# A hybrid decoder layer on one core: DRAM copies issued one behind each weight load, adding transfers one block to a step, and operand splits tied to places between products

## The chip, the cores and the metric

The kernel runs on one core of one Trainium2 chip. The metric is device time in microseconds, from the launch to the last instruction's end. The kernel before was timed in three runs: 650.31, 654.16 and 656.45 us, with a median of 654.16 us.

A core has five engines with a queue of instructions each, which run in the order of their queue and wait for each other by semaphores: TensorE (PE in the profile; its weight loads are PEld), VectorE (DVE), ScalarE (ACT), GpSimd (POOL) and SyncE (SP). SP only issues DMA transfers here; POOL and ACT issue some too.

## The reference

One layer over 512 tokens of width 1024, in float32:

```python
h = rms_norm(x, norm_g)
hq, hf, hi, hz, cq, ckv, kr, mz, glog = split(h @ w_in)
y_a = hgrn2(hq, hf, hi) with per-head rms_norm, * silu(hz)     # 8 heads of 128, chunks of 32
y_b = mla(cq, ckv, kr) * silu(mz)                              # 8 heads, causal softmax attention
gates = sigmoid(glog + b_gate)                                 # 512 x 2 x 1024
merged = gates[:, 0] * (y_a @ w_proj_a) + gates[:, 1] * (y_b @ w_proj_b)
x = x + merged @ w_out
return rms_norm(x, final_norm_g)
```

The 1024 x 1024 products for the two gates, for w_proj_a and for w_out are each done as seven products of half-size blocks instead of eight (a Strassen form). These need sums of weight blocks.

## The kernel before

**Precision.** A float32 operand is split into a high part (hi, rounded to the fast matmul type) and the rest (lo); each product is three matmuls, hi x hi, hi x lo and lo x hi. For weights, `load_w` (line 97) does this: SP issues the load of 512 KB into a raw buffer (three of them), ScalarE casts it to hi (line 113), VectorE subtracts to get lo (line 114); hi and lo have four buffers each. For other operands `split` (line 153) does the same two steps, and `a_parts` (line 826) calls it for two halves of a block.

**Stages.** First come the norm, the transposes and the small latent projections. Then four pairs of recurrent heads (`hg_pair`, line 562), each with weight loads for f (2), in every second pair i (4), q (2) and the gate z (2). In a pair, `hg_forget` and `hg_query` use VectorE and POOL, `hg_scores` and `hg_out` follow, and the norm's power runs on POOL. Then eight attention heads (line 893): scores with softmax, `mla_rope` for every second head, a gate, the next head's projections and the output. `mla_rope` (line 612) moves rows with DMAs from ScalarE's queue (qs<-qr, lines 618 and 625) with three POOL operations between. Its result qp is needed by the head's scores. Then come the two gates' products, the projection of branch a, all through `strassen` (line 867), then the projection of branch b, the product with w_out and the final norm.

**Block sums.** Class `BlockSums` (line 726) makes the weight sums in DRAM. For each of four matrices (the two gates', w_proj_a and w_out) there are four sum tensors t[0] to t[3] (g_t, pa_t and out_t in the profile). `start` (line 734) copies a block of the matrix into each, as two DRAM-to-DRAM transfers of 512 KB on SP's queue: eight to a matrix, 32 in all. `add` (line 740) adds a block or an earlier sum to one or more of them with adding transfers that POOL issues, two to a sum, 32 in all. t[0] and t[2] add blocks; t[1] adds t[0], and t[3] adds t[1].

**Where these stand.** `beside` (line 797) starts the first gate's copies after pair 0, the second's after pair 1 and pa's after pair 2; w_out's start with head 1 (line 920). The table `steps` (line 787) puts adds behind the f or q part of a pair (`step("f", pair)`, `step("q", pair)`) or behind a head (`step("h", h)`), with the sums 0 and 2 together. Six steps with adds lie in the pairs and six at the heads 1 to 6.

**The order.** The framework's scheduler orders each engine's instructions by its own model of their times. Inside `tc.manual_schedule` the named engines keep the order of the program. `tc.issue_after(ins)` makes the instructions traced in its block, of the engine that runs `ins`, stand behind `ins` in that engine's queue, with no wait. In `start`, these are the copies behind the last weight load traced; in `add`, POOL's issues behind `last_pool`, the last POOL operation of a head that has been noted.

**The gate stage.** Once the heads are done, the first gate's `strassen` runs (line 954). The branch's operands y11, y12 and y22 are then split into q1, q2 and q3, and four differences of blocks are made in `ya` (lines 955 to 962). The second gate's `strassen` has four more splits between its products (line 967), which write s1 to s4 once the products have read them. After it, eight splits of `yb` go into the space of hT (line 971), and the projection of branch a follows (line 981).

Of the kernel before, what the change touches and what calls it, by code (L numbers as in the profile page):

```python
# [9 lines left out]
F32 = mybir.dt.float32  # L10
# [4 lines left out]
ALU = mybir.AluOpType  # L15
# [8 lines left out]
H = 8  # L24
# [14 lines left out]
def hybrid_layer(ctx: ExitStack, tc: tile.TileContext, a):  # L39
# [55 lines left out]
    last_dma = [None]  # L95

    def load_w(*pieces, to=None):

        raw = wraw.tile([P, WCH], F32, tag="raw", name="w_raw")
        hi, lo = to or [pool.tile([P, WCH], F32R, tag=tag, name=f"w_{tag}")[:] for pool, tag in ((whi, "hi"), (wlo, "lo"))]  # L100
        views, o = [], 0
        for src in pieces:
            n = int(np.prod(src.shape[1:]))
            if len(src.shape) == 4:
                _, k, h, c = src.shape
                dst = raw[:, o : o + n].rearrange("p (k h c) -> p k h c", k=k, h=h)
                for i in range(k):
                    nc.sync.dma_start(dst[:, i], src[:, i])
            else:
                last_dma[0] = nc.sync.dma_start(raw[:, o : o + n].rearrange("p (k c) -> p k c", k=src.shape[1]), src)  # L110
            views.append([t[:, o : o + n].rearrange("p (k c) -> p k c", k=src.shape[1]) for t in (hi, lo)])
            o += n
        nc.scalar.copy(hi[:, :o], raw[:, :o])  # L113
        nc.vector.tensor_tensor(lo[:, :o], raw[:, :o], hi[:, :o].bitcast(F32), op=ALU.subtract)  # L114
        return views[0] if len(views) == 1 else views
# [42 lines left out]
    def power(out, x, mul, add, expo):  # L158

        nc.gpsimd.tensor_scalar(out, x, mul, add, op0=ALU.mult, op1=ALU.add)  # L160
        nc.gpsimd.tensor_tensor(out, out, expo, op=ALU.pow)
# [369 lines left out]
    def hg_out(h, asb, st_, q128, v_sb):  # L531
# [11 lines left out]
        power(ss[:], ss[:], 1.0 / P, 4 * EPS, neg_half)  # L543
# [18 lines left out]
    def hg_pair(pair, before_gate=None, last=None):  # L562
# [3 lines left out]
        step("f", pair)  # L566
# [15 lines left out]
        step("q", pair)  # L582
# [8 lines left out]
        def outs(aa):  # L591
            return [hg_out(h, aa[i], sts[i], qq[i][2], v_sb) for i, h in enumerate(hs)]
# [133 lines left out]
    class BlockSums:  # L726
# [7 lines left out]
        def start(self):  # L734
            with tc.issue_after(last_dma[0].ins):
                for t, ij in zip(self.t, TERMS):
                    for q in kh:
                        nc.sync.dma_start(t[:, q], self.w[ij][:, q])
# [22 lines left out]
    def early_sums(q):  # L761
# [9 lines left out]
        def keep(n, tag, src):  # L771
            hl = [ma_pool.tile([P, 2, 256], F32R, f"{tag}{i}") for i in range(2)]
            split(hl[0][:], hl[1][:], src)
            for i in range(2):
# [12 lines left out]
    steps = {("f", 0): lambda: early_sums(kh[0]),  # L787
             ("f", 1): lambda: gate_w[0].add(0, 2), ("q", 1): lambda: gate_w[0].add(1), ("f", 2): lambda: gate_w[0].add(3),
             ("q", 2): lambda: gate_w[1].add(0, 2), ("f", 3): lambda: gate_w[1].add(1), ("q", 3): lambda: gate_w[1].add(3),
             ("h", 1): lambda: pa_w.add(0, 2), ("h", 2): lambda: pa_w.add(1), ("h", 3): lambda: pa_w.add(3),  # L790
             ("h", 4): lambda: out_w.add(0, 2), ("h", 5): lambda: out_w.add(1), ("h", 6): lambda: out_w.add(3)}

    def step(*at):
        if at in steps:
            steps[at]()

    def beside(pair):
        if pair < 2:
            gate_w[pair].start()
        if pair == 0:  # L800
            early_sums(kh[1])
        if pair == 2:
            pa_w.start()

    for pair in range(H // 2 - 1):
        hg_pair(pair)
        beside(pair)
# [59 lines left out]
    def strassen(w, ops, out, pool, first=None, between={}):  # L867

        y11, y12, y22, s1, s2, s3, s4 = ops
        run = lambda n: between[n]() if n in between else None  # L870
        if first is None:
            u = ch_product(w.block(0, 0), y11, copied("c11", 1.0, pool))
            ch_product(w.block(1, 0), y12, closed("c11", 0, 0, 1.0, out), tile=mm_tile)
        else:
            u = first
# [17 lines left out]
    for h in range(H):  # L893
# [22 lines left out]
        elif h:  # L916
            late = (h, hook(), v, z)
            step("h", h)
            if h == 1:
                out_w.start()  # L920
        else:
            with tc.manual_schedule(engines={mybir.EngineType.PE}):
                nope = mla_nope(1, pools[1])
                v = mla_values(0)
                late = (0, hook(), v, z)
# [26 lines left out]
    h_ops = (h11, h12, h22, s1, s2, s3, s4)  # L952
    with tc.manual_schedule(engines={mybir.EngineType.PE}):
        strassen(gate_w[0], h_ops, gate_out(0, lambda j: ma[:, j]), gp, first=u)
    y11, y12, y21, y22 = blocks(ya)
    for y, q in ((y11, q1), (y12, q2), (y22, q3)):
        a_parts(y, q)
    for q in kh:
        minus(y22[:, q], y22[:, q], y21[:, q])
        minus(y21[:, q], y11[:, q], y21[:, q])  # L960
        minus_minus(y11[:, q], y22[:, q], y11[:, q])
        minus_minus(y12[:, q], y12[:, q], y11[:, q])
# [3 lines left out]
    with tc.manual_schedule(engines={mybir.EngineType.PE}):  # L966
        strassen(gate_w[1], h_ops, gate_out(1, lambda j: g1[j]), gp,
                 between={3: lambda: a_parts(y22, s1), 4: lambda: a_parts(y11, s2), 5: lambda: a_parts(y12, s4),
                          6: lambda: a_parts(y21, s3)})
    ybs = hT  # L970
    for h in range(H):
        split(ybs[0][:, h], ybs[1][:, h], yb[:, h])
# [7 lines left out]
    with tc.manual_schedule(engines={mybir.EngineType.PE}):  # L980
        strassen(pa_w, (q1, q2, q3, s1, s2, s3, s4), gated, gp)
# [203 lines left out]
```

## Time and profile before

| | us |
|---|---|
| median of the runs | 654.16 |
| lowest and highest run | 650.31, 656.45 |
| the profiled execution | 655.34 |
| its span, first to last instruction | 653.2 |
| TensorE busy in the span | 614.3 |
| VectorE, ScalarE, POOL busy | 431.2, 285.0, 143.8 |

The profile is one execution. A digit of its slices is a busy share in tenths of a 40th of the span, some 16 us; PEclk is the clock granted to TensorE in tenths of full speed. A row of a timeline gives the start and the duration in us, engine, line, operation, out<-in, the count, and in brackets the idle time of the engine before it and what ended it. "ACTq" or "SPq" marks the engine's sequencer, which issues DMAs. Line numbers are those of the kernel before.

### The profile page before, as it was taken

The page shows a single profiled execution, that of the slowest core. Times are in us where ns is not written, and L with a number is a line of the kernel's source. Part 1 is how long each engine was busy: PE and PEld are TensorE (multiplying, and loading weights), DVE is VectorE, ACT ScalarE, POOL GpSimd, SP SyncE. Part 2 cuts the span into 40 slices and gives each one's busy share as a digit, 9 for nine tenths or more (in the row PEclk, how much of TensorE's full clock was granted, in tenths as well). Part 3 has the DMA queues.
Part 4 walks back from the last instruction along what each step waited for, and adds up shares of the span by engine and source line. Part 5 has one row for each costly group of instructions (what it writes and reads, how often), then busy time and mean ns, then how long its engine had stood idle before and what let it go on. Part 6 is the DMA issues. An engine that isn't in the chain of part 4 may idle for free.

```text
span 653.2 us, 9792 instructions
## 1 busy us (share of the span) xinstructions
PE 614.3 (94%) x3688; PEld 534.9 (82%) x3688; DVE 431.2 (66%) x679; ACT 285.0 (44%) x531; POOL 143.8 (22%) x245
## 2 busy tenths in 40 slices
PE   8999999999999799939999997998999999999994
PEld 5998888878888588828887786887999999988884
DVE  7728987776944468527573864567746776667785
ACT  5554433332232233244542553446467754333453
POOL 3115340335414034321352344130000000000002
PEclk9999999999999899978999997999899999999999
DMA  7424399949599714980479778295656555684143
GB/s 251 148 76 153 113 276 338 325 140 187 136 235 281 173 33 92 243 273 15 116 129 190 165 133 193 71 276 175 193 194 189 178 180 176 204 306 156 33 129 128
DMA packets 74799, 114.37 MB, mean 175 GB/s; under 512 B 7512, under 2 KB 41726, under 8 KB 74752
## 3 DMA queue, kind: packets, MB, share of 16 engines
q1 hardware_dynamic: 65100, 89.69, 43.6%
q0 software_dynamic: 7952, 21.50, 17.4%
q10 hardware_dynamic: 1700, 2.56, 1.2%
q8 instruction: 29, 0.48, 0.3%
q14 instruction: 18, 0.15, 0.1%
HBM read 105.34 MB, written 39.85 MB: 222 GB/s over the span
## 4 chain that ended last, share of the span: by engine, by line
PE 43%; DMA 9%; DVE 5%; ACT 3%; issue 2%; POOL 2%; ACTq 0%; POOLq 0%; SPq 0%; DVEq 0%
PE ax_ps L840 15%; PE mm_ps L91 7%; PE mm_ps L92 7%; PE mm_ps L93 6%; DMA qs<-qr 3%; DMA w_raw<-w_ukv 3%; PE mm_ps L840 3%; DMA out_t<-w_out 2%; DVE w_lo L114 1%; DMA w_raw<-w_in 1%; PE ax_ps L677 1%; PE ax_ps L701 1%; DVE ya L1057 1%; ACT w_hi L113 1%; PE ax_ps L91 1%
## 5 line engine op out<-in xcount | busy, mean ns | idle before, releaser
L114 DVE TENSOR_TENSOR w_lo<-w_raw,w_hi 128x1024 fp32r<-128x1024 f32 (+3 forms) x116 | 135.2, 1180 | 106.9 <-ACT w_hi L113 101.4
L113 ACT CAST w_hi<-w_raw 128x1024 fp32r<-128x1024 f32 (+3 forms) x116 | 114.7, 1005 | 133.0 <-DMA w_raw<-w_in 37.5
L91 PE MATMUL mm_ps<-hT,w_hi 128*128 128x512 f32 x320 | 126.3, 396 | 0.5 <-ACT tf L449 0.5
L92 PE MATMUL mm_ps<-hT,w_hi 128*128 128x512 f32 x320 | 125.4, 392 | 0.0
L93 PE MATMUL mm_ps<-hT,w_lo 128*128 128x512 f32 x320 | 124.9, 392 | 0.0
L91 PEld LDWEIGHTS mm_ps<-hT,w_hi 128*128 128x128 f32 x320 | 60.3, 189 | 13.3 <-ACT tf L449 0.9
L93 PEld LDWEIGHTS mm_ps<-hT,w_lo 128*128 128x128 f32 x320 | 60.2, 188 | 12.3
L92 PEld LDWEIGHTS mm_ps<-hT,w_hi 128*128 128x128 f32 x320 | 60.3, 188 | 11.7
L840 PE MATMUL ax_ps<-s,w_hi 128*128 128x256 f32 x384 | 55.8, 289 | 2.1 <-ACT w_hi L113 2.1
L840 PEld LDWEIGHTS ax_ps<-s,w_hi 128*128 128x128 f32 x384 | 51.2, 197 | 2.5 <-ACT w_hi L113 2.5
L1075 POOL TENSOR_SCALAR ssum<-ssum 128x1 f32<-128x1 f32 x3 | 1.0, 317 | 189.3 <-ACT sq L1062 189.3
L93 PE MATMUL mm_ps<-w_hi,hT 128*128 128x512 f32 (+1 forms) x96 | 36.7, 384 | 0.0
L92 PE MATMUL mm_ps<-w_lo,hT 128*128 128x512 f32 (+1 forms) x96 | 36.5, 382 | 0.0
L91 PE MATMUL mm_ps<-w_hi,hT 128*128 128x512 f32 (+1 forms) x96 | 36.4, 386 | 0.0
L840 PE MATMUL ax_ps<-s,w_lo 128*128 128x256 f32 x192 | 32.5, 291 | 1.1 <-DVE w_lo L114 1.1
L683 ACT ACTIVATE p<-ax_ps,sm 128x128 f32<-128x128 f32 (+3 forms) x32 | 16.9, 530 | 29.6 <-DVE sm L682 26.3
L685 POOL TENSOR_SCALAR p<-p,sm 128x128 f32<-128x128 f32 (+3 forms) x28 | 16.2, 583 | 60.8 <-DVE sm L684 46.3
L840 PEld LDWEIGHTS ax_ps<-s,w_lo 128*128 128x128 f32 x192 | 27.6, 199 | 1.6 <-DVE w_lo L114 1.6
L455 DVE RECIPROCAL tf<-pr 128x512 f32<-128x512 f32 x8 | 26.8, 3349 | 0.2
L156 DVE TENSOR_TENSOR pt<-ax_ps,pt 128x512 fp32r<-128x512 f32 (+1 forms) x24 | 13.7, 591 | 14.1 <-ACT pt L155 14.1
L91 PE MATMUL mm_ps<-cT,w_hi 128*128 128x512 f32 x52 | 20.8, 399 | 0.0
L93 PEld LDWEIGHTS mm_ps<-w_hi,hT 128*128 128x128 f32 x96 | 18.0, 188 | 3.0
(296 smaller groups left out, 1223.5 us busy)
## 6 DMA issues: line engine op xcount, KB each, us to landing
w_raw<-w_in SPq DMA_DIRECT2D x54, 512.0 KB, 7.6
g_t<-w_in SPq DMA_DIRECT2D x16, 512.0 KB, 12.7
w_raw<-g_t SPq DMA_DIRECT2D x16, 512.0 KB, 4.6
g_t<-w_in POOLq DMA_DIRECT2D x8, 512.0 KB, 13.0
g_t<-g_t POOLq DMA_DIRECT2D x8, 512.0 KB, 9.5
pa_t<-w_proj_a SPq DMA_DIRECT2D x8, 512.0 KB, 11.2
out_t<-w_out SPq DMA_DIRECT2D x8, 512.0 KB, 13.4
s<-h POOLq DMA_DIRECT2D x8, 512.0 KB, 7.1
```

The lines of the kernel that those rows point to most:

```text
L91: nc.tensor.matmul(ps, lh[lsl], rh[rsl], start=start, stop=False)
L92: nc.tensor.matmul(ps, lh[lsl], rl[rsl], start=False, stop=False)
L93: nc.tensor.matmul(ps, ll[lsl], rh[rsl], start=False, stop=stop)
L113: nc.scalar.copy(hi[:, :o], raw[:, :o])
L114: nc.vector.tensor_tensor(lo[:, :o], raw[:, :o], hi[:, :o].bitcast(F32), op=ALU.subtract)
L156: nc.vector.tensor_tensor(lo, src, hi.bitcast(F32), op=ALU.subtract)
L455: nc.vector.reciprocal(rp[:], pr[:])
L677: nc.tensor.matmul(sps[:, :n], qh[:, bl], kpe[x][:, :n], start=False, stop=x == 1)
L683: nc.scalar.activation(p[:, :n], sps[:, :n], AF.Exp, scale=SCALE, bias=sm[:, 1:2], accum_out=sm[:, 2:3])
L685: scaled_p = (nc.vector if final else nc.gpsimd).tensor_scalar(p[:, :n], p[:, :n], sm[:, 3:4], 0.5, op0=ALU.mult, op1=ALU.mult)
L701: nc.tensor.transpose(tps[b][:, c : c + P], pn[i][:, j * P : j * P + P], ident[:])
L840: nc.tensor.matmul(ps[:, o], w[k // 2][i][:, k % 2, cols], ap[j][:, k], start=not banks and c == 0 and n == 0, stop=n == 11, skip_group_ch ...
```

## The change

Copies: `start` no longer issues anything; it puts its eight copies into a list, `queued`. All four matrices are started before pair 0. Each weight load with a three-dimensional source then takes one copy off the list and issues it right behind itself on SP.

Adds: a list of 16 adds and one empty place, one sum each (two transfers), replaces the table. `step()` takes the next. It is called at q and after the outputs in pair 0, at f, at q and after the outputs in pairs 1 to 3, and at the heads 1 to 6: 17 places. At f of pair 0 the early sums stay. `power` returns its last operation, and a head's norm notes it as `last_pool`, so that an add after the outputs stands behind it.

Splits: what `strassen` runs between products is placed behind the last lo subtraction on VectorE, and there are two more places, after the first and the second product. The first gate's products now have the splits of y11, y12 and y22 and a difference between them, the second gate's the other differences beside the splits they had, and the projection of branch a the eight splits of `yb`.

```diff
@@ load_w
                 last_dma[0] = nc.sync.dma_start(raw[:, o : o + n].rearrange("p (k c) -> p k c", k=src.shape[1]), src)
+                if queued:
+                    with tc.issue_after(last_dma[0].ins):
+                        queued.pop(0)()
...
-        nc.vector.tensor_tensor(lo[:, :o], raw[:, :o], hi[:, :o].bitcast(F32), op=ALU.subtract)
+        last_lo[0] = nc.vector.tensor_tensor(lo[:, :o], raw[:, :o], hi[:, :o].bitcast(F32), op=ALU.subtract)
@@ hg_out
-        power(ss[:], ss[:], 1.0 / P, 4 * EPS, neg_half)
+        last_pool[0] = power(ss[:], ss[:], 1.0 / P, 4 * EPS, neg_half)
@@ hg_pair
-        step("f", pair)
+        if pair:
+            step()
+        else:
+            early_sums(kh[0])
...
-        step("q", pair)
+        step()
...
         def outs(aa):
-            return [hg_out(h, aa[i], sts[i], qq[i][2], v_sb) for i, h in enumerate(hs)]
+            on = [hg_out(h, aa[i], sts[i], qq[i][2], v_sb) for i, h in enumerate(hs)]
+            step()
+            return on
@@ BlockSums
         def start(self):
-            with tc.issue_after(last_dma[0].ins):
-                for t, ij in zip(self.t, TERMS):
-                    for q in kh:
-                        nc.sync.dma_start(t[:, q], self.w[ij][:, q])
+            for t, ij in zip(self.t, TERMS):
+                for q in kh:
+                    queued.append(lambda t=t[:, q], w=self.w[ij][:, q]: nc.sync.dma_start(t, w))
@@ steps
+    adds = [(gate_w[0], 0), (gate_w[0], 2), (gate_w[0], 1), (gate_w[1], 0), (gate_w[0], 3), (gate_w[1], 2), (gate_w[1], 1),
+            (pa_w, 0), (gate_w[1], 3), (pa_w, 2), (pa_w, 1), (out_w, 0), (pa_w, 3), (out_w, 2), (out_w, 1), None, (out_w, 3)]
+
+    def step():
+        if adds and last_pool[0]:
+            x = adds.pop(0)
+            if x:
+                x[0].add(x[1])
+
+    for w in (*gate_w, pa_w, out_w):
+        w.start()
@@ strassen
-        run = lambda n: between[n]() if n in between else None
+        def run(n):
+            if n in between:
+                with tc.issue_after(last_lo[0].ins):
+                    between[n]()
...
             u = ch_product(w.block(0, 0), y11, copied("c11", 1.0, pool))
+            run(1)
             ch_product(w.block(1, 0), y12, closed("c11", 0, 0, 1.0, out), tile=mm_tile)
+            run(2)
@@ gate stage
-        strassen(gate_w[0], h_ops, gate_out(0, lambda j: ma[:, j]), gp, first=u)
-    y11, y12, y21, y22 = blocks(ya)
-    for y, q in ((y11, q1), (y12, q2), (y22, q3)):
-        a_parts(y, q)
...
+        strassen(gate_w[0], h_ops, gate_out(0, lambda j: ma[:, j]), gp, first=u,
+                 between={3: lambda: a_parts(y11, q1), 4: lambda: a_parts(y12, q2), 5: lambda: a_parts(y22, q3),
+                          6: lambda: [minus(y22[:, q], y22[:, q], y21[:, q]) for q in kh]})
...
-                 between={3: lambda: a_parts(y22, s1), 4: lambda: a_parts(y11, s2), 5: lambda: a_parts(y12, s4),
-                          6: lambda: a_parts(y21, s3)})
+                 between={1: lambda: [minus(y21[:, q], y11[:, q], y21[:, q]) for q in kh],
+                          2: lambda: [minus_minus(y11[:, q], y22[:, q], y11[:, q]) for q in kh],
+                          3: lambda: [a_parts(y22, s1)] + [minus_minus(y12[:, q], y12[:, q], y11[:, q]) for q in kh],
+                          4: lambda: a_parts(y11, s2), 5: lambda: a_parts(y12, s4), 6: lambda: a_parts(y21, s3)})
...
-        strassen(pa_w, (q1, q2, q3, s1, s2, s3, s4), gated, gp)
+        strassen(pa_w, (q1, q2, q3, s1, s2, s3, s4), gated, gp,
+                 between={1: lambda: y_split(0), 2: lambda: y_split(1), 3: lambda: y_split(2, 3), 4: lambda: y_split(4, 5),
+                          5: lambda: y_split(6), 6: lambda: y_split(7)})
```

More of the change, by code (lines that the diff above doesn't have):

```diff
@@ L95, in hybrid_layer @@
     last_dma = [None]
+    last_lo = [None]
+    queued = []
     def load_w(*pieces, to=None):
@@ L160, in power @@
         nc.gpsimd.tensor_scalar(out, x, mul, add, op0=ALU.mult, op1=ALU.add)
-        nc.gpsimd.tensor_tensor(out, out, expo, op=ALU.pow)
+        return nc.gpsimd.tensor_tensor(out, out, expo, op=ALU.pow)
     cT = [cpool.tile([P, 5, S], F32R, f"cT{i}") for i in range(2)]
@@ L785, in early_sums @@
         keep(4, "qn", e12)
[L787 to L799, printed above, removed]
+    adds = [(gate_w[0], 0), (gate_w[0], 2), (gate_w[0], 1), (gate_w[1], 0), (gate_w[0], 3), (gate_w[1], 2), (gate_w[1], 1),
[7 more added lines that the diff above has]
+        w.start()
+    for pair in range(H // 2 - 1):
+        hg_pair(pair)
         if pair == 0:
             early_sums(kh[1])
[L802 to L807, printed above, removed]
     early = []
@@ L917, in hybrid_layer @@
             late = (h, hook(), v, z)
-            step("h", h)
-            if h == 1:
-                out_w.start()
+            step()
         else:
@@ L952, in hybrid_layer @@
     h_ops = (h11, h12, h22, s1, s2, s3, s4)
+    y11, y12, y21, y22 = blocks(ya)
     with tc.manual_schedule(engines={mybir.EngineType.PE}):
-        strassen(gate_w[0], h_ops, gate_out(0, lambda j: ma[:, j]), gp, first=u)
-    y11, y12, y21, y22 = blocks(ya)
-    for y, q in ((y11, q1), (y12, q2), (y22, q3)):
-        a_parts(y, q)
[L958 to L962, printed above, removed]
+        strassen(gate_w[0], h_ops, gate_out(0, lambda j: ma[:, j]), gp, first=u,
+                 between={3: lambda: a_parts(y11, q1), 4: lambda: a_parts(y12, q2), 5: lambda: a_parts(y22, q3),
+                          6: lambda: [minus(y22[:, q], y22[:, q], y21[:, q]) for q in kh]})
     g1 = {j: z_tile()[:] for j in (0, 1, 4)}
@@ L967, in hybrid_layer, with y_split @@
         strassen(gate_w[1], h_ops, gate_out(1, lambda j: g1[j]), gp,
-                 between={3: lambda: a_parts(y22, s1), 4: lambda: a_parts(y11, s2), 5: lambda: a_parts(y12, s4),
-                          6: lambda: a_parts(y21, s3)})
+                 between={1: lambda: [minus(y21[:, q], y11[:, q], y21[:, q]) for q in kh],
+                          2: lambda: [minus_minus(y11[:, q], y22[:, q], y11[:, q]) for q in kh],
+                          3: lambda: [a_parts(y22, s1)] + [minus_minus(y12[:, q], y12[:, q], y11[:, q]) for q in kh],
+                          4: lambda: a_parts(y11, s2), 5: lambda: a_parts(y12, s4), 6: lambda: a_parts(y21, s3)})
     ybs = hT
-    for h in range(H):
-        split(ybs[0][:, h], ybs[1][:, h], yb[:, h])
+    def y_split(*heads):
+        for h in heads:
+            split(ybs[0][:, h], ybs[1][:, h], yb[:, h])
     def gated(j, tok, src):
```

## The prediction, made before the changed kernel was built or run

> **What bounds the kernel now.** The page first, to learn which engine sets the time and when it is not busy.
>
> ```profile
> span 653.2 us, 9792 instructions
> PE 614.3 (94%) x3688; PEld 534.9 (82%) x3688; DVE 431.2 (66%) x679; ACT 285.0 (44%) x531; POOL 143.8 (22%) x245
> PE   8999999999999799939999997998999999999994
> PEclk9999999999999899978999997999899999999999
> DMA  7424399949599714980479778295656555684143
> ```
>
> TensorE sets the time: it is idle for 653.2 - 614.3 = 38.9 us, and most of that lies in few slices, where the granted clock falls as well. The change adds and removes no matmul, so it can only move these 38.9 us and the slow clock behind them. Next the busy time by stretches cut around the gaps (columns: length, busy us of PE, PEld, DVE, ACT and POOL, granted clock, DMA share, GB/s), and, from two finer cuts, the stretches of slow clock.
>
> ```profile
> 60.00:220.00 160.00, 159.23 (x962) 132.49 (x961) 117.37 (x144) 50.80 (x95) 50.97 (x90) 1.00 0.81 222
> 220.00:232.00 12.00, 7.33 (x37) 6.70 (x36) 4.05 (x6) 4.10 (x12) 0.60 (x2) 0.72 0.30 88
> 225.00:230.00 5.00, 3.77 (x18) 3.80 (x19) 2.23 (x4) 0.35 (x2) 0.00 (x0) 0.50 0.17 39
> 281.00:300.00 19.00, 7.61 (x30) 6.59 (x29) 6.67 (x13) 7.30 (x24) 2.45 (x4) 0.64 0.61 191
> 295.00:300.00 5.00, 5.00 (x19) 4.48 (x18) 2.13 (x8) 0.46 (x2) 0.00 (x0) 0.58 0.16 35
> 345.00:365.00 20.00, 17.05 (x88) 13.72 (x88) 9.15 (x25) 8.14 (x19) 5.46 (x8) 1.00 0.82 185
> 395.00:405.00 10.00, 6.20 (x27) 5.44 (x26) 3.51 (x5) 2.49 (x4) 7.11 (x6) 0.66 0.73 178
> 400.00:405.00 5.00, 5.00 (x18) 4.61 (x19) 1.17 (x2) 0.96 (x2) 4.10 (x4) 0.50 0.86 161
> 448.00:465.00 17.00, 13.81 (x88) 12.89 (x87) 13.73 (x19) 10.75 (x18) 0.00 (x0) 0.80 0.47 144
> 460.00:465.00 5.00, 5.00 (x32) 5.00 (x32) 3.23 (x5) 2.24 (x3) 0.00 (x0) 0.69 0.76 257
> 465.00:560.00 95.00, 95.00 (x793) 95.00 (x793) 63.19 (x78) 60.23 (x91) 0.00 (x0) 1.00 0.56 180
> 635.00:653.20 18.20, 9.96 (x55) 8.24 (x53) 11.07 (x20) 5.87 (x16) 4.54 (x10) 0.93 0.29 115
> ```
>
> Each gap costs its idle time and then busy time at a low clock (busy time x the part of the clock that is missing):
> - A, 220 to 232: 12.00 - 7.33 = 4.7 idle, 3.77 x 0.50 = 1.9 of clock: 6.6 us.
> - B, 281 to 300: 19.00 - 7.61 = 11.4 idle, 5.00 x 0.42 = 2.1 of clock: 13.5 us.
> - C, 345 to 365: 20.00 - 17.05 = 2.9 us, clock full.
> - D, 395 to 405: 3.8 idle, 5.00 x 0.50 = 2.5 of clock: 6.3 us.
> - E, 448 to 465: 17.00 - 13.81 = 3.2 idle, some 3.0 of clock (1.5 in its last 5 us, as much assumed before them): 6.2 us.
>
> These are 35.5 us. The last 18.20 us hold 8.2 us more, which the change leaves alone. From 60 to 220 us and from 465 to 560 us TensorE hardly waits. Next, what ends each gap, by the timeline of each engine.
>
> ```profile
> 222.10 1.04 ACT L113 CAST w_hi<-w_raw 128x1024 fp32r<-128x1024 f32 x1 [4.79 <-DMA w_raw<-w_in]
> 223.18 1.22 DVE L114 TENSOR_TENSOR w_lo<-w_raw,w_hi 128x1024 fp32r<-128x1024 f32 x1 [3.54 <-ACT w_hi L113]
> 226.23 1.19 PE L536 MATMUL ax_ps<-v,asb 128*128 128x128 f32 x4 [4.67 <-DVE asb L527]
> 264.06 1.90 ACTq L618 DMA_DIRECT2D qs<-qr  x3
> 268.58 12.03 SPq L738 DMA_DIRECT2D out_t<-w_out  x8
> 274.67 1.27 POOL L619 TENSOR_TENSOR qr<-qr,qtab 128x512 f32<-128x512 f32 x1 [5.43 <-DMA qs<-qr]
> 277.25 1.27 POOL L621 TENSOR_TENSOR qr<-qr,qs 128x512 f32<-128x512 f32 x1
> 280.70 4.82 ACTq L625 DMA_DIRECT2D qs<-qr  x2
> 285.56 1.24 ACT L630 CAST qp<-qr 64x512 fp32r<-64x512 f32 x2 [15.20 <-DMA qs<-qr]
> 294.42 0.79 PE L91 MATMUL mm_ps<-w_hi,cT 128*128 128x512 f32 x1 [11.39 <-DVE z L558]
> 331.75 18.02 DMA w_raw<-w_ukv
> 377.87 4.64 POOL L745 DMA_DIRECT2D out_t<-w_out  x4
> 385.64 2.48 ACTq L618 DMA_DIRECT2D qs<-qr  x4
> 396.99 1.26 POOL L619 TENSOR_TENSOR qr<-qr,qtab 128x512 f32<-128x512 f32 x1 [5.95 <-DMA qs<-qr]
> 399.95 1.11 PE L701 MATMUL ax_ps<-ident,p 128*128 128x128 f32 x4 [3.80 <-POOL p L685]
> 449.40 3.21 ACT L155 CAST q<-ya 128x512 fp32r<-128x512 f32 x6
> 450.09 3.70 DVE L156 TENSOR_TENSOR q<-ya,q 128x512 fp32r<-128x512 f32 x6 [1.50 <-ACT q L155]
> 453.00 1.98 ACT L113 CAST w_hi<-w_raw 128x1024 fp32r<-128x1024 f32 x2
> 454.08 0.51 PE L840 MATMUL ax_ps<-s,w_hi 128*128 128x256 f32 x2 [1.61 <-ACT w_hi L113]
> ```
>
> A: a weight load lands late, ScalarE and VectorE wait for it in their order, and the score copy behind them holds TensorE. B: the rope transfers qs<-qr take from 264.06 to 274.67, their second pair starts at 280.70 though POOL was done at 277.25 + 1.27 = 278.5, ScalarE stands for 15.20 us, and the gate's z behind it holds TensorE. The eight copies into out_t run beside this. C and D: a weight load of 18.02 us and rope transfers that end at 396.99, with adding transfers under way. E: six operand splits stand ahead of the weight splits on ScalarE and VectorE. Last, how long transfers take by company (issue to landing).
>
> ```profile
> w_raw<-w_in SPq DMA_DIRECT2D x7, 512.0 KB, 13.0
> g_t<-g_t POOLq DMA_DIRECT2D x4, 512.0 KB, 9.8
> qs<-qr ACTq DMA_DIRECT2D x4, 64.0 KB, 3.7
> qs<-qr ACTq DMA_DIRECT2D x4, 64.0 KB, 8.5
> ```
>
> These are the weight loads of 185 to 222 us, the adding transfers of 125 to 185 us, and the rope transfers of a quiet stretch (282 to 330 us) and of D's (380 to 402 us).
>
> **The change part by part.**
>
> Copies. The 32 copies of 512 KB stay; each is now issued on SP behind one weight load from the first pair on. Counting load_w's calls: ten go with pair 0, six with pair 1, ten with pair 2, six with pair 3, so all are out with pair 3's last load, ahead of the first rope transfer at 264.06. Before, 24 were issued ahead of the out_t burst at 268.58 and eight in it. So 60 to 220 us gets at most eight copies more and loses bursts. From the row of 60 to 220 us, 222 GB/s at a share of 0.81 make 274 GB/s at a full share: a copy takes 0.524 MB / 274 GB/s = 1.9 us of all DMA engines, eight take 15 us, and the share rises by 0.10. With two adds more (below) it stays near 0.95. The cover is that loads landed in 13.0 us at the median in 185 to 222 us while TensorE ran on until 221.6. I cost it at nothing there, with an upper bound of one gap like A, 6.6 us.
> For B it takes the eight copies away. The rope's first group then still has adds beside it (a step at pair 3's q is left): 10.6 us before, 3.7 when quiet, I take 8. The wait of 280.70 - 278.5 = 2.2 us goes. The second pair of transfers takes 4.8 and may take 3.7. Together 2.6 + 2.2 + 1.1 = 5.9 us, and with part of the clock 7. Ends: 2.2 us (only the wait) and 13.5 us (all of B). What is late next is the row of ScalarE work behind qp, from 286.8 to z at 294.4, which stays; so I don't take all.
> For A, 8 copies and 4 adds beside these loads become 6 and 2. But the order on VectorE, with the score copy behind a weight split, is the scheduler's and may stay. Ends 0 and 6.6, taken 3.5.
>
> Adds. The 32 adds stay, and also 4 to a step become 2. Eleven steps lie in the pairs instead of six, so 22 adds run there instead of 16, and 10 instead of 16 beside the attention heads. The step at the fifth head has none. For D, four adds were issued from 377.87 and were still landing when the rope's transfers ran; two, at 9.8 us each, are done by 390. The rope then ends some 4 us sooner, as much as TensorE waited (3.80), and without that gap the 2.5 us of clock go too: ends 0 and 6.3, taken 4.5. For C, two adds in place of four lie beside the load of 18.02 us: ends 0 and 2.9, taken 1.5. On POOL, an add's issue costs 4.64 / 4 = 1.2 us; in the pairs six more are 7 us, spread over 230 us of an engine that is busy for 22%. The new ones behind a pair's norms stand ahead of the next pair's forget chain: 2 x 1.2 = 2.4 us, hidden by the projection that runs then; without that cover up to 2.4 us each, three times.
>
> Pins. The VectorE half of each split now follows the second weight split of the product just issued; its ScalarE half is not bound. The six splits (3.70 us) are spread over three products, so weight splits wait for at most two (1.2 us). The ScalarE casts (3.21 us) can still run in one piece, and then the wait of 1.61 us stays. E's ends: 1.6 us (what of the 3.2 idle is not that wait) and 6.2 us, taken 3.5. In the second gate and the projection that follows, the same splits move by some products; VectorE has 95 - 63.19 = 31.8 us free there, so they cost nothing; a pin that comes at a bad place costs its pair of splits, 1.2 to 1.4 us.
>
> New gaps. The orders of all engines are made anew, and a new wait of A's or C's size can turn up at any place. Ends 0 and 10, taken 4.
>
> Sum: 3.5 + 7 + 1.5 + 4.5 + 3.5 - 4 = 16 us. The profiled execution took 655.34 us, 1.2 us above the median of 654.16; 655.3 - 16 = 639.3, so 638 to 639 against the median. I say 639.
>
> One rule bears on B and D. The Trainium skill, "DMA: Bandwidth & Descriptors", section Queues, rings and completion order, says that each DMA engine takes turns between the queues that have work, packet by packet. By that rule rope transfers on ScalarE's queue don't stand behind SP's copies, and fewer adds help only once none is in flight; the second rival below works this out.
>
> **The rivals.**
>
> Adds in the way of POOL (slower). Place: the three steps behind the pairs' outputs. There the issue, and a wait for an earlier block's transfer, stand ahead of the next forget chain, from which scores and states come. It decides once POOL is held for longer than the projection beside it, some 48 matmuls or 10 us. For it: adds that build on sums need up to 9.8 us to land. Against it: each builds on a block whose step is one or more earlier. If it comes, three gaps like A on top of the gains: 639 + 3 x 6.6 + 4 (no C, D gain either, as POOL makes the rope) = 663.
>
> Sharing, not queueing (no change). The rope's transfers share the DMA engines with POOL's adds whether two or four are queued, and only the wait for out_t goes from B. Then A 0, B 2.2, C 0, D 2, E 1.6, new gaps 0 to 4: 655.3 less 2 to 6, near 651. For it: the first group took 10.6 us though the copies began only at 268.58. Against it: 3.7 us in the quiet stretch. By the rule above this is what taking turns gives, and the trace bears it out only in part.
>
> Nearly everything goes (faster). If the order on ScalarE behind qp and VectorE's order at A change with the transfers, A to E go but for 6 us: 655.3 - 29 = 626.
>
> **How the numbers follow.** Forecast and its neighbours (628 to 647) 0.62; nearly everything 0.08; sharing, within 1% of the time before, 0.18; POOL or new gaps, 0.12. Less than 1% (6.5 us) can hardly be told from no change. Faster by over 1% (below 647.6) thus 0.70, same 0.18, slower 0.12. The range reaches from 628 to 655, where the second rival ends: some 7% lie below it and 13% above. The forecast's own range is 628 to 647.
>
> **What would show it.** Right: no SP burst of eight copies, weight loads before 220 us landing in under 13 us, B's gap below 6 us and rope transfers there done in 8 us or less, no gap near 396, granted clock 1.00 through the gate stage. Wrong: a gap at 220 or 282 of the old length with the copies gone (then it was order, not transfers), POOL waiting behind a pair's norms, or a gap ahead of 220 us where there was none (then the copies starve the loads). The 8.2 us at the end should stay as they are.

## The result and the profile after

| | before | changed |
|---|---|---|
| median of the runs | 653.45 us (650.31 to 656.45) | 627.40 us (626.55 to 628.44) |
| profiled execution, its span | 655.34, 653.2 us | 626.55, 624.8 us |

The ratio is 0.9603, with a 95% interval of 0.9554 to 0.9651. The change takes 26 us off. The forecast of 639 had the direction right and the size too small; the time lies 0.6 us below the range's low end. The kernel before has one run more here than ahead of the prediction, 652.74 us, which moves its median from 654.16 to 653.45. One execution of undo_copies (853.71 us) and one of undo_adds (2119.21 us), two kernels of the experiments below, were disturbed, and their ratios leave these out.

The page of the changed kernel, with the lines that were shown of the kernel before (line numbers in the rows from here on are those of the kernel that each fence names):

```profile
span 624.8 us, 9801 instructions
PE 603.7 (97%) x3688; PEld 526.9 (84%) x3688; DVE 431.9 (69%) x679; ACT 284.6 (46%) x531; POOL 147.7 (24%) x245
PE   8999999999999999979998999898999999999994
PEclk9999999999999999999999999999999999999998
DMA  7449479988979944937575662584656555685043
```

The span is 28.4 us shorter. TensorE's idle time went from 38.9 to 624.8 - 603.7 = 21.1 us, so 17.8 us came from gaps. Its busy time, for the same matmuls, went from 614.3 to 603.7, so 10.6 us came from the clock: no slice before the end is below 9. VectorE, ScalarE and POOL run as many instructions as before; VectorE and ScalarE are busy for as long within 0.7 us, POOL for 3.9 us longer.

The next view is the busy time by stretches, cut around the places where A to E were (columns as in the prediction):

```profile
60.00:220.00 160.00, 160.00 (x974) 134.58 (x973) 120.98 (x150) 53.04 (x97) 53.32 (x93) 1.00 0.87 241
215.00:268.00 53.00, 53.00 (x336) 45.08 (x335) 36.68 (x47) 15.10 (x35) 20.40 (x37) 1.00 0.64 135
268.00:285.00 17.00, 12.71 (x70) 10.21 (x70) 8.57 (x21) 8.34 (x28) 7.89 (x10) 1.00 0.42 76
320.00:345.00 25.00, 23.29 (x126) 19.64 (x125) 15.75 (x33) 11.53 (x26) 10.90 (x12) 1.00 0.65 127
380.00:420.00 40.00, 38.35 (x243) 34.60 (x242) 24.28 (x61) 18.76 (x39) 9.11 (x14) 1.00 0.60 188
420.00:440.00 20.00, 17.70 (x140) 16.99 (x139) 12.14 (x15) 12.76 (x20) 0.00 (x0) 1.00 0.51 165
606.60:624.80 18.20, 9.74 (x54) 8.07 (x52) 10.71 (x19) 5.87 (x16) 4.54 (x10) 0.88 0.29 116
```

In the first stretch, where the single copies went, the DMA share rose from 0.81 to 0.87 and TensorE was busy for all 160.00 us. The last 18.20 us are idle for 8.5 us, as before (8.2). The rest answers to the prediction's terms:

| | was | left | gained | forecast |
|---|---|---|---|---|
| A | 6.6 | 0 | 6.6 | 3.5 |
| B | 13.5 | 17.00 - 12.71 = 4.3 | 9.2 | 7 |
| C | 2.9 | 25.00 - 23.29 = 1.7 | 1.2 | 1.5 |
| D | 6.3 | 0 | 6.3 | 4.5 |
| E | 6.2 | 20.00 - 17.70 = 2.3 | 3.9 | 3.5 |
| new gaps | | 0.6 | -0.6 | -4 |

The new gap is the 1.65 us idle in the stretch from 380 to 420, at 403; the kernel before had some 1.0 us at the same step. These sum to 26.6 us; the other 1.8 us of the span lie in gaps and dips too short to list.

What ends the gaps that are left stands in the timelines of TensorE, POOL, ScalarE and VectorE (start, duration, engine, line, operation, and in brackets the idle time and what ended it):

```profile
255.09 1.90 ACTq L628 DMA_DIRECT2D qs<-qr  x3
256.15 2.35 POOL L754 DMA_DIRECT2D pa_t<-w_proj_a  x2 [0.17 <-issue]
267.12 1.26 POOL L629 TENSOR_TENSOR qr<-qr,qtab 128x512 f32<-128x512 f32 x1 [8.62 <-DMA qs<-qr]
269.68 1.28 POOL L631 TENSOR_TENSOR qr<-qr,qs 128x512 f32<-128x512 f32 x1
271.00 1.17 ACTq L635 DMA_DIRECT2D qs<-qr  x2
272.21 1.25 ACT L640 CAST qp<-qr 64x512 fp32r<-64x512 f32 x2 [11.89 <-issue]
276.56 0.44 PE L687 MATMUL ax_ps<-kpe,qp 128*128 128x128 f32 x2 [2.51 <-DVE qp L641]
282.18 0.50 PE L91 MATMUL mm_ps<-w_hi,cT 128*128 128x512 f32 x1 [1.07 <-DVE z L563]
338.16 0.55 PE L711 MATMUL ax_ps<-ident,p 128*128 128x128 f32 x3 [1.36 <-POOL p L695]
403.37 0.41 PE L91 MATMUL ax_ps<-kn,qn 128*128 128x384 f32 x1 [1.61 <-DVE pt L161]
424.49 3.21 ACT L160 CAST q<-ya 128x512 fp32r<-128x512 f32 x6
425.18 1.29 DVE L161 TENSOR_TENSOR q<-ya,q 128x512 fp32r<-128x512 f32 x2 [1.50 <-ACT q L160]
429.17 0.50 PE L844 MATMUL ax_ps<-s,w_hi 128*128 128x256 f32 x2 [1.61 <-ACT w_hi L118]
431.43 1.28 DVE L161 TENSOR_TENSOR q<-ya,q 128x512 fp32r<-128x512 f32 x2
```

And the transfers of the rope at B (issue to landing), first of the kernel before (260 to 290 us):

```profile
qs<-qr ACTq DMA_DIRECT2D x4, 64.0 KB, 6.1
qs<-qr ACTq DMA_DIRECT2D x2, 128.0 KB, 8.2
```

Then of the changed kernel (250 to 275 us):

```profile
qs<-qr ACTq DMA_DIRECT2D x4, 64.0 KB, 7.2
qs<-qr ACTq DMA_DIRECT2D x2, 128.0 KB, 2.3
```

At B the rope's first group is no faster without copies beside it: 267.12 - 255.09 = 12.0 us, where it had 10.6. Adding transfers run beside both: here two that POOL issues at 256.15, behind two at 249.61, and in the kernel before four from 257.00 to 268.43. In only_copies (below), with the adds as before and no copies beside it, it takes 265.37 - 254.73 = 10.6 us. The second pair starts at 271.00, right as POOL's 269.68 + 1.28 ends, where it had waited for 2.2 us. Its issue takes 1.17 us instead of 4.82, and it lands in 2.3 us instead of 8.2. ScalarE's cast of qp reads qr and not these transfers, but stands behind their issue in its queue: it starts at 272.21, behind 271.00 + 1.17, as it started at 285.56 behind 280.70 + 4.82. From the cast of qp to the gate's z and TensorE's row behind it there are still 282.18 - 272.21 = 10.0 us (294.42 - 285.56 = 8.9 before). What is new is TensorE's order. The row that waits for z stood first there, ahead of the scores of qp; now these scores stand first, so that TensorE has work in between and waits 2.51, 0.67 and 1.07 us, not 11.39. At E, VectorE's splits come in pairs behind the weight splits, as the pins say, but ScalarE's six casts still run in one piece of 3.21 us, and the wait of 1.61 us behind them stays.

### The profile page after: what moved, and what is told of

Same layout as the page of the kernel before. It is cut to its first block, busy times and chain, and to the rows that moved or that the text cites. A ratio compares the mean times of both kernels' runs of the same rounds, so it can differ in the third digit from the quotient of the medians.

```text
span 624.8 us, 9801 instructions
## 1 busy us (share of the span) xinstructions
PE 603.7 (97%) x3688; PEld 526.9 (84%) x3688; DVE 431.9 (69%) x679; ACT 284.6 (46%) x531; POOL 147.7 (24%) x245
## 4 chain that ended last, share of the span: by engine, by line
PE 78%; DVE 8%; DMA 4%; ACT 4%; issue 3%; POOL 2%; ACTq 0%; POOLq 0%; SPq 0%; DVEq 0%
PE mm_ps L91 16%; PE mm_ps L92 16%; PE mm_ps L93 16%; PE ax_ps L844 16%; PE mm_ps L844 3%; DMA qs<-qr 2%; DVE w_lo L119 2%; PE mm_ps L271 1%; PE ax_ps L687 1%; PE ax_ps L711 1%; DMA w_raw<-w_uq 1%; DVE ya L1067 1%; PE ax_ps L541 1%; PE ax_ps L91 1%; PE ax_ps L93 1%
## 5 line engine op out<-in xcount | busy, mean ns | idle before, releaser
L119 DVE TENSOR_TENSOR w_lo<-w_raw,w_hi 128x1024 fp32r<-128x1024 f32 (+3 forms) x116 | 137.1, 1194 | 91.2 <-ACT w_hi L118 85.4
L844 PE MATMUL ax_ps<-s,w_hi 128*128 128x256 f32 x384 | 54.2, 283 | 2.1 <-ACT w_hi L118 2.1
L844 PEld LDWEIGHTS ax_ps<-s,w_hi 128*128 128x128 f32 x384 | 49.6, 192 | 2.5 <-ACT w_hi L118 2.5
L844 PEld LDWEIGHTS ax_ps<-s,w_lo 128*128 128x128 f32 x192 | 26.6, 192 | 0.4 <-DVE w_lo L119 0.4
L93 PEld LDWEIGHTS mm_ps<-w_hi,hT 128*128 128x128 f32 x96 | 18.0, 188 | 3.0
L91 PEld LDWEIGHTS mm_ps<-w_hi,hT 128*128 128x128 f32 x96 | 18.0, 188 | 3.0
```

The source lines that it names most:

```text
L91: nc.tensor.matmul(ps, lh[lsl], rh[rsl], start=start, stop=False)
L93: nc.tensor.matmul(ps, ll[lsl], rh[rsl], start=False, stop=stop)
L119: last_lo[0] = nc.vector.tensor_tensor(lo[:, :o], raw[:, :o], hi[:, :o].bitcast(F32), op=ALU.subtract)
L844: nc.tensor.matmul(ps[:, o], w[k // 2][i][:, k % 2, cols], ap[j][:, k], start=not banks and c == 0 and n == 0, stop=n == 11, skip_group_ch ...
```

## The experiments

Each ratio is to runs of the kernel before on the same chip.

| kernel | median us | ratio, 95% interval |
|---|---|---|
| changed kernel | 627.40 | 0.9603, 0.9554 to 0.9651 |
| undo_copies | 652.15 | 0.9966, 0.9940 to 0.9993 |
| undo_adds | 630.98 | 0.9654, 0.9607 to 0.9702 |
| undo_pins | 630.31 | 0.9654, 0.9609 to 0.9699 |
| only_copies | 633.39 | 0.9702, 0.9663 to 0.9740 |
| only_pins | 649.82 | 0.9940, 0.9894 to 0.9985 |
| out_burst_earlier | 656.82 | 1.0040, 1.0004 to 1.0075 |
| bursts_on_pool | 648.25 | 0.9924, 0.9890 to 0.9959 |
| two_behind_a_load | 630.11 | 0.9647, 0.9569 to 0.9726 |
| four_behind_a_load | 632.97 | 0.9676, 0.9607 to 0.9745 |
| bursts_same_order | 660.58 | 1.0086, 1.0059 to 1.0113 |
| singles_burst_order | 630.07 | 0.9613, 0.9577 to 0.9649 |
| singles_order_of_before | 644.22 | 0.9827, 0.9790 to 0.9865 |
| casts_tied_too | 624.81 | 0.9565, 0.9525 to 0.9605 |

### What each part is worth

The changed kernel with its copies in bursts of eight again, one matrix ahead of each pair:

```diff
         def start(self):
-            for t, ij in zip(self.t, TERMS):
-                for q in kh:
-                    queued.append(lambda t=t[:, q], w=self.w[ij][:, q]: nc.sync.dma_start(t, w))
+            with tc.issue_after(last_dma[0].ins):
+                for t, ij in zip(self.t, TERMS):
+                    for q in kh:
+                        nc.sync.dma_start(t[:, q], self.w[ij][:, q])
...
-    for w in (*gate_w, pa_w, out_w):
-        w.start()
+    gate_w[0].start()
     for pair in range(H // 2 - 1):
         hg_pair(pair)
+        (gate_w[1], pa_w, out_w)[pair].start()
```

> The changed kernel with the copies in bursts of eight again, but placed so that the new adds find them done: the first gate's before pair 0, the second gate's after pair 0, pa's after pair 1, w_out's after pair 2. Everything else as in the changed kernel (627.4 us). Theory 1 (one copy behind each load keeps the loads on time): the gap near 220 us comes back, idle and slow clock, 6.6 us: 634 us, with weight loads of 12 us or more beside the last burst. Rival (what counted was only that w_out's eight copies left the rope transfers near 270 us, and bursts elsewhere cost nothing): 627 to 629 us, no gap near 215.

It took 652.15 us, so the theory and the rival were both far off: with bursts again, nearly all of what the change brings is lost. With `steps` and the sums of 0 and 2 together again, and everything else as changed:

> The changed kernel with the adds at their old places, two sums together and four transfers to a step; copies and pins as changed. Theory 1 (each part of the change has its own gaps, and adds have C and D): 2.9 + 6.3 us come back, less what is left of C now (1.7): some 7.5 us, 635 us, with a gap near 370 us (D, rope transfers of 9 us beside four adds) and slow clock behind it. Rival (C and D went because the orders of the engines were made anew): 627 to 630 us, no gap at D's place.

It took 630.98 us. There is no gap near 396, so the rival has it for D. At C's step the gaps are longer (2.00 and 1.35 us), with a slower clock behind them:

```profile
335.00:345.00 10.00, 6.65 (x27) 5.63 (x26) 4.69 (x8) 4.24 (x9) 6.65 (x7) 0.68 0.57 120
```

This stretch costs 3.4 us of idle time and 6.65 x 0.32 = 2.1 of clock, where 1.7 us in all are left in the changed kernel. With the gate stage's splits again as before:

> The changed kernel with the gate stage as before: splits not tied to places. Theory 1: E's wait on VectorE and the slow clock behind it come back, 3.9 us: 631 us, granted clock near 0.65 for some 8 us behind 430 us. Rival (the clock's slow stretch at E came by chance, not with the longer wait): 628 to 629 us, only the 0.9 us of idle more.

It took 630.31 us. A gap of 0.88 us ended by w_lo is back behind the two of E, and so is the slow clock:

```profile
418.00:438.00 20.00, 17.05 (x113) 16.21 (x112) 15.03 (x21) 10.82 (x18) 0.00 (x0) 0.83 0.50 162
```

That is 3.0 us idle and 17.05 x 0.17 = 2.9 of clock, against 2.3 us in all in the changed kernel; theory 1 holds for this profile. The two kernels lie at 0.9654 where the changed one lies at 0.9603: about 3 us each, at the edge of what these intervals tell apart. Next the kernel before with one part alone, the copies (`load_w` and `start` as changed) or the pins (`strassen` and the gate stage as changed):

> The kernel before with the copies alone changed: one behind each weight load. Theory 1 (parts add up; copies have A and B): 6.6 + 9.5 us less than before: 637 to 638 us, no gap at A, B at some 4 us, C, D and E as before. Rival (parts don't add up, since each new order has gaps of its own): above 643 us or below 633 us.

> Kernel before, with the pinned splits alone. If the three parts add up (copies 21, adds 3, pins 2.5 to 3 as found by putting each back), this is 650 to 651 us with the gap at 454 shorter by some 1 us and no slow clock behind it. If putting the copies first changed what the pins are worth, 653 to 655 us.

The copies alone gave 3.0% or 19 us, against an expectation of 637 to 638: the theory was too small, and the rival's high side fell, while its low side, 633, is 0.39 us away, too little to decide. Gaps A and D are gone in it, D with four adds to a step as before. One gap grew, at the second rope:

```profile
335.51 1.27 POOL L624 TENSOR_TENSOR qr<-qr,qtab 128x512 f32<-128x512 f32 x1 [1.26 <-DMA qs<-qr]
337.98 1.45 POOL L690 TENSOR_SCALAR p<-p,sm 128x256 f32<-128x256 f32 x1
339.48 0.69 PE L706 MATMUL ax_ps<-ident,p 128*128 128x128 f32 x2 [4.82 <-POOL p L690]
```

That is TensorE's and POOL's timeline of only_copies: POOL makes the rope while a softmax row p queues behind it. In the changed kernel 1.36 us are left of that gap. The pins alone gave 0.6% or 4 us. Copies 3.0%, pins 0.6% and the adds' 0.5% sum to 4.1%, beside 4.0% for the change: the parts add up, as far as intervals of some 0.4% each way can tell.

### What a burst does

One more execution of undo_copies shows where its time goes.

> The same kernel as undo_copies (652 us, and its profile did not fall into an undisturbed run), for a profile alone. Theory 1a (each burst of eight holds up the weight loads and rope transfers that are issued behind it): gaps of 5 us or more within 40 us behind each burst, loads there at 12 us or more to landing, 20 us of idle and slow clock more than in the changed kernel. Rival (the engines' new orders cost it, wherever the bursts are): gaps with no late transfer in front of them.

It took 649.34 us, with 33.1 us idle and some 10 us of slow clock. Four gaps are new, and their releasers differ: 3.10 us at 87.5 (w_lo, behind VectorE's own differences), 2.58 at 123.8 (asb), 1.38 at 152.7 (z) and 4.83 at 228.8 (a late load). None reaches the 5 us that theory 1a asked for. The first ends before the second gate's burst, which is issued from 87.88 on, and a like gap of 2.39 us is there with single copies in this kernel's order (singles_burst_order, below), so most of it is order. The others could be either, as the engines' orders had been made anew. Three kernels vary the burst. First w_out's eight copies right behind pa's eight, in the kernel before:

> The kernel before with one edit: the eight copies of w_out start after pair 2, right behind pa's eight, instead of with head 1. Theory 1a: B shrinks by the wait for out_t and more (its rope transfers get at most 8 us), 7 to 10 us less, but sixteen copies in a row make A longer by the eight copies' 15 us of transfers, as loads stand behind them: together 655 to 663 us. Rival 2 (what counts is that nothing bursts beside the rope): B gone, A as it was: 643 to 646 us.

```profile
183.06 0.37 SPq L110 DMA_DIRECT2D w_raw<-w_in  x1
183.47 7.07 SPq L738 DMA_DIRECT2D pa_t<-w_proj_a  x8
191.31 17.23 SPq L738 DMA_DIRECT2D out_t<-w_out  x8
208.63 31.55 SPq L110 DMA_DIRECT2D w_raw<-w_in  x5
233.91 1.04 ACT L113 CAST w_hi<-w_raw 128x1024 fp32r<-128x1024 f32 x1 [21.91 <-DMA w_raw<-w_in]
235.01 0.80 PE L91 MATMUL mm_ps<-hT,w_hi 128*128 128x512 f32 x1 [20.85 <-ACT w_hi L113]
```

These are SP's, ScalarE's and TensorE's timelines of it: the load issued behind sixteen copies starts at 208.63, 25.6 us after the one ahead of the copies, and TensorE stands for 20.85 us. B falls to 2.41 us, but the burst only moved the wait. It took 656.82 us. Then the bursts of the kernel before on POOL's queue:

```diff
-            with tc.issue_after(last_dma[0].ins):
+            with tc.issue_after(last_pool[0].ins):
...
-                        nc.sync.dma_start(t[:, q], self.w[ij][:, q])
+                        nc.gpsimd.dma_start(t[:, q], self.w[ij][:, q])
```

> The kernel before with its bursts of copies issued by POOL instead of SP, behind the last noted POOL operation; adds and splits as before. Theory 1a (the loads queue behind copies on SP's own queue): without copies on that queue A goes and B loses the wait for out_t, 640 to 645 us. Rival 3 (the copies take the DMA engines' time whichever queue they are on, or hold POOL): no gain, 652 us or more.

```profile
329.90 0.69 POOL L738 DMA_DIRECT2D out_t<-w_out  x1 [3.14 <-DMA pa_t<-w_proj_a]
331.06 1.13 PE L701 MATMUL ax_ps<-ident,p 128*128 128x128 f32 x3 [5.12 <-POOL p L685]
```

It took 648.25 us, between the two expectations. A is gone and 2.7 us are left at B, but POOL waits for transfers that are under way before it issues a copy (3.14 us in the first row) and the softmax behind it holds TensorE for 5.12 us. A gap of 3.15 us at 178.92 is new, too: behind copies that POOL issues until 171.7, VectorE waits 9.36 us for POOL's part of the forget chain. So the rival "POOL in the way" is real, for the copies. The Trainium skill, "DMA: Bandwidth & Descriptors", section Queues, rings and completion order, says that DMA engines take turns between queues, packet by packet; this case agrees: the weight loads between 60 and 240 us, on SP's queue, land in 5.4 us at the median with the bursts on POOL's, and in 11.4 us in the kernel before. Last, in the changed kernel, more than one copy behind each load until the list is empty:

```diff
                     with tc.issue_after(last_dma[0].ins):
-                        queued.pop(0)()
+                        for _ in range(2):      # four_behind_a_load: range(4)
+                            queued.pop(0)()
```

> Changed kernel, but two copies go behind each of the first 16 weight loads instead of one behind each of 32. Theory (what counts is how long a weight load stands behind copies on SP's queue): each load now has 1 MB of copies ahead of it instead of 0.5 MB; the loads keep some slack, so 627 to 633 us, with no gap over 2 us that the changed kernel lacks. Rival (what counts is only that the copies lie where the scheduler's order of the engines was made without bursts; any spacing will do, and early copies are as good): 626 to 628 us.

> Changed kernel, but four copies go behind each of the first 8 weight loads, so that all 32 are issued in pair 0. Theory: a load stands behind 2 MB of copies, some 8 us of all DMA engines at 274 GB/s, eight times; the loads of pair 0 land late and TensorE waits there, 3 to 8 us a time in some of the eight places: 635 to 660 us, with the new gaps between 25 and 110 us. Rival: 626 to 630 us, as the three raw buffers hold the loads far enough ahead.

They took 630.11 and 632.97 us: two fits its theory but for a gap of 2.20 us at 127, and four lies between the theory's 635 and the rival's 630. Even with all 32 copies issued in pair 0, no gap in the four pairs is over 1.73 us. So what counts is how many copies stand in one piece ahead of a load. The sizes fit one estimate of mine: at 1.9 us a copy (the prediction's figure), four hold a load for 8 us, eight for 15 and sixteen for 30; with gaps of at most 1.73, of 4.83 (and up to 10.94 below) and of 20.85 us behind them the loads have some 5 to 10 us of slack.

### Transfers or order

The scheduler makes the engines' orders anew when copies move, so three kernels hold them fixed: each instruction of TensorE, VectorE, ScalarE and GpSimd is tied behind the one that precedes it in the order of another kernel, and only SP's queue differs. ORDER, a table in the kernel that is not shown here, holds that order.

```diff
+    traced = nc.cur_bb.bb.instructions
+    for name, runs in ORDER.items():
+        mine = [i for i in traced if i.engine == getattr(mybir.EngineType, name)]
+        order = [mine[k] for o, n in runs for k in range(o, o + n)]
+        for i, j in zip(order, order[1:]):
+            tc.add_manual_dep(j, i.name, mybir.DependencyInfo(mybir.DependencyClass.NoSync, mybir.DependencyReason.DATA),
+                              reason="order")
```

> Copies in bursts of eight as in undo_copies, but every instruction of TensorE, VectorE, ScalarE and GpSimd held in the order that the changed kernel has. Theory 1 (the bursts themselves make loads late): 643 to 652 us, with gaps of 3 to 5 us behind the bursts near 97, 130 and 205, ended by weight splits whose load was late. Theory 2 (the orders that the scheduler made for the bursts cost the time): 627 to 634 us, no gap over 2 us behind a burst.

> One copy behind each load as in the changed kernel, but the four engines held in the order that undo_copies has. Theory 1: 627 to 633 us. Theory 2: 642 to 652 us, with the gaps near 87 and 124 as in undo_copies. Both in part: 633 to 642 us; then the two shares are read from this run and the one beside it.

> Kernel before, with one copy behind each load and nothing else changed, the four engines held in the order of the kernel before (only_copies had its orders made anew: 633.4 us). Theory 1: 633 to 640 us, gaps A and B gone or under 5 us. Theory 2: 645 to 653 us, A and B as before, as VectorE and ScalarE have the same rows ahead of the score copy and of z.

| copies, order of the four engines | ratio |
|---|---|
| single, of the changed kernel (the changed kernel) | 0.9603 |
| single, of undo_copies | 0.9613 |
| bursts, of undo_copies | 0.9966 |
| bursts, of the changed kernel | 1.0086 |

With either order the bursts cost 23 to 32 us (3.5% and 4.8% of 654), and with single copies the two orders are the same within their intervals; that also says that tying the engines to another order costs nothing that shows. Theory 1 holds, and undersized the first run (652 us at most, 660.58 measured): the order made for the bursts had even hidden 8 us of them. The timelines of SP, ScalarE and TensorE in bursts_same_order show the loads:

```profile
84.31 0.38 SPq L120 DMA_DIRECT2D w_raw<-w_in  x1
84.74 0.57 SPq L756 DMA_DIRECT2D g_t<-w_in  x1
...
94.62 6.72 SPq L120 DMA_DIRECT2D w_raw<-w_in  x3
106.27 1.04 ACT L126 CAST w_hi<-w_raw 128x1024 fp32r<-128x1024 f32 x1 [16.67 <-DMA w_raw<-w_in]
109.83 0.80 PE L99 MATMUL mm_ps<-hT,w_hi 128*128 128x512 f32 x1 [10.94 <-DVE f L494]
...
155.37 0.80 PE L99 MATMUL mm_ps<-hT,w_hi 128*128 128x512 f32 x1 [5.29 <-ACT tf L462]
...
231.68 0.80 PE L99 MATMUL mm_ps<-hT,w_hi 128*128 128x512 f32 x1 [7.57 <-DVE f L494]
```

The load behind the second gate's burst is issued at 94.62, ten us after the one ahead of it, and cast at 106.27; ScalarE has waited for 16.67 us and TensorE waits for 10.94. The gaps behind three bursts sum to 23.8 us. In this kernel the loads between 60 and 240 us landed in 10.7 us at the median, in the changed one in 8.0.

The third kernel splits the gain another way. Single copies with the order of the kernel before give 1.7%, or 11 us; letting the scheduler order the engines anew (only_copies) gives another 1.3%, or 8 us. Its gaps say which is which. A is gone with the old order:

```profile
215.00:270.00 55.00, 53.70 (x337) 45.04 (x336) 39.58 (x50) 15.46 (x36) 16.45 (x36) 1.00 0.67 157
270.00:290.00 20.00, 13.40 (x69) 11.67 (x68) 8.75 (x21) 8.81 (x30) 5.72 (x8) 0.83 0.21 51
395.00:405.00 10.00, 7.38 (x25) 5.88 (x24) 5.86 (x14) 3.64 (x6) 0.00 (x0) 0.71 0.20 56
282.61 0.80 PE L99 MATMUL mm_ps<-w_hi,cT 128*128 128x512 f32 x1 [6.59 <-DVE z L571]
```

In its stretches and TensorE's timeline, B keeps 6.59 us idle and some 2 us of clock, and D keeps 2.6 us and its slow clock. Theory 1 had the place of A right and the size too large (633 to 640 expected, 644.22 measured); theory 2's 645 is within the lowest and highest run. Both are at work here.

### Can the last gap of E go

The changed kernel, with ScalarE's casts of the pinned splits tied too:

```diff
-        nc.scalar.copy(hi[:, :o], raw[:, :o])
+        last_hi[0] = nc.scalar.copy(hi[:, :o], raw[:, :o])
...
-                with tc.issue_after(last_lo[0].ins):
+                with tc.issue_after(last_lo[0].ins), tc.issue_after(last_hi[0].ins):
```

> The changed kernel with the ScalarE casts of the tied splits placed behind the product's last hi cast as well. Theory 1: the six casts no longer run in one piece ahead of the weight casts, so the waits of 1.61 and 0.45 us near 429 us go: 625 to 626 us. Rival (other work stands there in their place): no change, 627 to 628 us.

```profile
425.90 1.13 ACT L161 CAST q<-ya 128x512 fp32r<-128x512 f32 x2
427.42 1.98 ACT L119 CAST w_hi<-w_raw 128x1024 fp32r<-128x1024 f32 x2
420.00:440.00 20.00, 19.51 (x156) 18.97 (x156) 13.79 (x17) 12.77 (x21) 0.00 (x0) 1.00 0.59 195
```

ScalarE's casts now come in pairs and TensorE is idle for 0.5 us of these 20, where it had 2.3. It took 624.81 us (623.55 to 626.05), as theory 1 expected; its interval overlaps the changed kernel's, so the gap is shown to go and the gain of some 2 us is likely, not shown.

## Why the prediction was off

What the copies do was forecast rightly in kind; what failed is the place of the engines' orders in it. The forecast took TensorE's order at B as given and priced new orders as a loss of 4 us, and in the runs they were a gain of some 8.

- **Copies over 60 to 220 us at nothing**: right. TensorE did not wait. The DMA share rose by 0.06 to 0.87, not by the 0.10 and more that the sum gave (near 0.95).
- **A, 3.5 of 6.6**: mechanism right, too small. The doubt was that the order on VectorE might keep it; with the old order held and single copies it is gone, so it was the load behind pa's burst, whole.
- **B, 7 of 13.5**: of its three terms the first (2.6, a faster first group) didn't come: with no copies and one step of adds beside it the group took 12.0 us, where 8 were forecast. The second (2.2, the wait) came. The third (1.1, the second pair) misread its row: 4.82 us at 280.70 is the time in which ScalarE's queue issued two transfers, not their time to land, which was 8.2 us. This issue, which held the cast of qp, went from 4.82 to 1.17 us, so that 3.7 us went where 1.1 were forecast. The step "what is late next is the row of ScalarE work behind qp, from 286.8 to z at 294.4, which stays; so I don't take all" failed. The row does stay (10.0 us in the changed kernel). With the old order it holds TensorE for 6.59 us, as the forecast supposed; with the new orders TensorE has the scores of qp ahead of the row that waits for z, and 9.2 us went. What failed is the step from a late row on ScalarE to a gap on TensorE of that length: it took TensorE's order as given.
- **D, 4.5 of 6.3, and C**: D went whole, but not through the adds. It is gone in only_copies, with four adds to a step, and stays, at less, where the copies are single and the order is the old one. So the re-made orders took the rest. The thinner adds earn their 3 us or so at C's step: without them it costs 5.5 us (undo_adds), with them 1.7. C itself came near (1.2 of 1.5), but it hangs on the orders as well: with the copies alone its gap grows to 4.82 us.
- **E, 3.5**: right (3.9). The 1.61 us that ScalarE's casts leave were named, and tying them takes them away.
- **New gaps, -4**: the largest miss, 3.4 us; A's is the next. It priced the re-made orders as a loss with bounds 0 and 10; below nothing was not allowed for. With single copies the re-made orders were a gain of 8 us.

The likeliest sum was thus 3.1 + 2.2 + 1.8 + 0.4 + 3.4 - 0.3 = 10.6 us too small in its terms, and 1.8 us lie outside them. The rival "nearly everything goes" came, at 626 against 627.4. Its condition was that the order on ScalarE behind qp and VectorE's order at A change with the transfers. It came in another way: ScalarE's row behind qp still takes 10.0 us, A goes with the old order held, and what changed at B is TensorE's order. So its number is in part luck. Its chance of 0.08 put the range's low end just above it. "Sharing, not queueing" was right on the rope's first group, which the copies did not hold up, and wrong on what decides: loads that stand behind copies in one queue. "Adds in the way of POOL" did not come.

## What to carry to other kernels

A bulk copy is best fed one piece behind each load that matters, since a load waits for the whole of what stands ahead of it in its queue; ask how much slack the loads have (here some 5 to 10 us) and keep each piece below it. When an edit moves transfers, a scheduler's new orders can be worth as much as the transfers; holding the old orders fixed in one run tells the two apart. A gap that ends on a slow chain goes either when the chain gets shorter or when the engine gets other work, so price both.

## What the runs showed that was not expected

A short gap is not always followed by a slow clock. The gap at the same step, 1.61 us ended by pt, is followed by full clock in the changed kernel and by a lower one in undo_copies_look; the rows are TensorE's timeline and the stretches, first of the changed kernel:

```profile
400.00:410.00 10.00, 8.36 (x57) 7.57 (x57) 8.62 (x26) 4.43 (x13) 3.43 (x7) 1.00 0.71 190
```

And of undo_copies_look:

```profile
423.33 0.41 PE L91 MATMUL ax_ps<-kn,qn 128*128 128x384 f32 x1 [1.61 <-DVE pt L161]
420.00:430.00 10.00, 8.35 (x45) 7.25 (x44) 7.53 (x24) 4.39 (x13) 2.16 (x4) 0.83 0.59 141
```

Busy for 8.35 us at 0.83, this one costs 1.4 us more. What decides it stays open; the clock part of a forecast for gaps of this length is uncertain by about their own length.

Issuing itself can stall: in out_burst_earlier SP took 7.07 us to issue the first eight copies and 17.23 us for the next eight, some 2 us each, about the 1.9 us that the prediction estimated for a copy on all DMA engines. A burst on SP's queue goes with such a stall on ScalarE's. In the two profiles with w_out's burst beside the first rope, the kernel before and only_pins, the second pair's issue starts 2.2 and 4.2 us after POOL is done and takes 4.82 and 2.90 us. In only_copies, bursts_on_pool and the changed kernel it starts within 0.1 us and takes 1.17. What links the two queues is not shown. Single copies are not free of it: two of the changed kernel's took SP 4.57 and 6.61 us to issue (at 110.12 and 154.25), with no gap on TensorE behind them.
